# Last FFN's second product in a hybrid trunk: one weight sum moved from DMA to VectorE, another order of work, two token tiles finished earlier

## The chip, the cores and the metric

The kernel runs on one core of a Trainium2 chip. The metric is the device time of one execution in microseconds, from the first to the last instruction and what lies around them; the number for a kernel is the median of several executions. The core has TensorE (PE in the profile, with its weight loads as PEld), VectorE (DVE), ScalarE (ACT), GpSimd (POOL) and SyncE (SP). They run side by side and wait for each other through semaphores. Each takes its own instructions strictly in program order, so an instruction that waits holds up all that stand behind it on the same engine. Transfers (DMA) can be issued from SP, ACT and POOL; only those issued from POOL add into their destination here.

## The reference, cut to what matters

Two layers, 512 tokens, 1024 features. Each layer has a mixer and a SwiGLU FFN, each between two RMS norms with shift, scale and gate. The change is in the last step of the last layer: the FFN's second matrix product, its norm, and the sum into `x`.

```python
D_MODEL = 1024; SEQ = 512; D_FF = 2816
def swiglu_ffn(h, w_in, w_out):
    gate, up = jnp.split(h @ w_in, 2, axis=-1)
    return (jax.nn.silu(gate) * up) @ w_out
...
        y = swiglu_ffn(h, f_w_in[i], f_w_out[i])
        x = x + gate * rmsnorm(y, norm_g[i, 3])
```

All matrix products are done to nearly float32 precision: each operand is split into a high part (a cast on ACT) and a low part (source minus high part, on DVE), and three matmuls stand for one (high by high, low by high, high by low).

## The kernel before, in words

The last second product, (512 x 2816) times (2816 x 1024), is done by a seven-product scheme of the Strassen-Winograd kind instead of eight. The 22 blocks of 128 hidden features are taken as 11 pairs `p`. In a pair the weight rows give four blocks: `b11`, `b12` (first row block, left and right 512 columns) and `b21`, `b22` (second row block). The activations give `a11`, `a12`, `a21`, `a22` (256 tokens each). The seven products, numbered 0 to 6 here, are in `PRODUCTS`, with the accumulator (a pair of PSUM banks `A`, `B`, `C` or `D`, one bank per 128 tokens), the weight block and the activation block:

```python
PRODUCTS = (("A", "b11", "a11"), ("B", "b21", "a12"), ("C", "b22", "a12"), ("A", "b22", "a11"),
            ("D", "b12", "s1"), ("A", "b11", "a21"), ("A", "b21", "a22"))
```

Each product runs over all 11 pairs, so there are 77 steps `(i, p)`, in the order of the list `steps`. Even products take the pairs in the order 0, 1, 2, ... (`even`), odd ones start with pair 4 (`odd`), since there the pairs 0 to 3 come in units of two. Two steps that follow each other make a tile `n`, so there are 39 tiles (0 to 38); a tile is 12 matmuls of 128x512 outputs (`products`, L1785). Tiles 0 to 5 are product 0, tiles 11 to 16 product 2, 16 to 21 product 3, 22 to 27 product 4, 27 to 32 product 5, and 33 to 38 product 6; where a product ends in mid-tile the next begins there. The last three tiles are done for the first 128 tokens of the half, and then for the second 128.

The blocks are changed in place between the products. A unit is a group of pairs that lie in one buffer: units 0 and 1 are the pairs (0, 1) and (2, 3) (512 KB in one block of both), units 2 to 8 the pairs 4 to 10 (256 KB each). The profile calls the buffers of units 0 to 2 `w2t`, those of units 3 and 4 `w2s`, and those of units 5 to 8 `w2h`. For each unit there are four weight sums:

- `t1`: `b12 += b11`, an accumulating DMA from POOL (L1626), before the loop over the tiles.
- `t2_`: `b22 += b12`, an accumulating DMA from POOL. It has to follow the casts of the old `b22` for product 2, and product 3 needs its result.
- `t3`: `b11` becomes the sum of the original `b12` and the original `b22`, for product 5. Before the change `t3_load` reads the original `b12` from memory again, by a DMA issued from ACT (L1796), and `t3` adds the original `b22` from memory by an accumulating DMA issued from POOL.
- `t4`: `b21 += b22`, an accumulating DMA from POOL, for product 6.

All instructions of this part stand in a written order on every engine. The loop over `n` issues `products([n])`, then `behind(n)` (weight sums and the reading of finished accumulators), then `w_prep(n + 4)` and `a_prep(n + 3)`. `w_prep` splits a tile's weights (ACT cast L1750, DVE subtraction L1751, four buffers `whlo`), `a_prep` splits its activations (ACT L1763, DVE L1764, three buffers `ao`). From `n` = 34 on `behind(n)` comes last. Because of the buffers, `w_prep(n + 4)` can start when PE has finished tile `n`.

The four results are read from the banks as products end: `c11` after product 0 and 1, `c12` after 2, 3 and 4 (at `n` = 27), `c22` after 4 and 5 (at `n` = 32, L2032, which has to read bank `A` before product 6 adds to it), and `c21` is what bank `A` holds at the end. `c11` and `c12` belong to the token tiles 0 and 1 of the output, `c21` and `c22` to the tiles 2 and 3. To finish a token tile, ACT squares the two halves and sums along the row (`square`, L1982), DVE forms a mean (`mean`), ACT takes the root and DVE the reciprocal (`root`, L1988 and L1989), DVE multiplies by the gate row (`gated`, L1992), and then forms the new `x` and a DMA stores it (`x_new`, L1998 and L1999).

Of the kernel before, what the change touches and what calls it, by code (L numbers as in the profile page):

```python
# [17 lines left out]
T = 512  # L18
D = 1024
# [12 lines left out]
MUL, ADD, SUB = ALU.mult, ALU.add, ALU.subtract  # L32
# [3 lines left out]
def trunk_kernel(  # L36
# [8 lines left out]
    dma_s = nc.scalar.dma_start  # L45
    act, dve, pe, pool = nc.scalar, nc.vector, nc.tensor, nc.gpsimd
# [16 lines left out]
    def t2(name):  # L63
        return tmp.tile([P, T], F32, tag="t2", name=name, bufs=4)
# [505 lines left out]
    with ExitStack() as ph:  # L570
# [112 lines left out]
        with tc.manual_schedule(engines={PE_ENGINE, mybir.EngineType.SP, mybir.EngineType.Activation,  # L683
# [215 lines left out]
            for k in range(18):  # L899
                i, jp = k % 6, 2 + k // 6 * 2  # L900
# [98 lines left out]
        with tc.manual_schedule(engines={PE_ENGINE, mybir.EngineType.SP, mybir.EngineType.Activation,  # L999
# [15 lines left out]
            for k in range(2 * NF - 6):  # L1015
# [8 lines left out]
                q, j = divmod(k - 3, 4)  # L1024
# [25 lines left out]
    with ExitStack() as ph:  # L1050
# [99 lines left out]
        class Group:  # L1150
# [169 lines left out]
            def root(self):  # L1320
                self.rg = t2("rg")
                act.activation(self.rg, self.ssg, AF.Sqrt, bias=eps_t, scale=1.0 / 256)
# [219 lines left out]
    with ExitStack() as ph:  # L1542
# [4 lines left out]
        NP = NF // 2  # L1547
# [5 lines left out]
        units = [(0, 1), (2, 3)] + [(p,) for p in range(4, NP)]  # L1553
        unit_of = {p: i for i, u in enumerate(units) for p in u}
        rows_of = {}

        def w2_rows(p, n=1):
            return w2[2 * p * P:(2 * p + 2 * n) * P, :].rearrange("(i c p) f -> p i c f", p=P, c=2)
# [10 lines left out]
        def w2_load(i, *names):  # L1569

            u = units[i]
            for name in names:
                r, c = int(name[1]) - 1, int(name[2]) - 1
                dma(b_(i, name), w2_rows(u[0], len(u))[:, :, r, c * T:(c + 1) * T])

        def b_(i, name, q=None):

            t = rows_of[i][int(name[1]) - 1][:, :, slice(0, T) if name[2] == "1" else slice(T, D)]
            return t if q is None else t[:, q, :]
# [45 lines left out]
        def add_(dst, src):  # L1625
            pool.dma_start(dst, src, accum_op=ADD)  # L1626
# [106 lines left out]

        even = list(range(NP))
        odd = [4, 0, 1, 2, 3] + list(range(5, NP))
        steps = [(i, p) for i in range(7) for p in (odd if i % 2 else even)]
        NT = (len(steps) + 1) // 2
        w_of, a_of = {}, {}

# [14 lines left out]
        def a_prep(n):  # L1754
            a = fo.tile([P, 2, 2, 256], F32R, tag="ao", name="ao")
            part = steps[2 * n:2 * n + 2]
            if len(part) == 2 and part[0][0] == part[1][0] and part[1][1] == part[0][1] + 1:
                todo = [(slice(0, 2), part[0], 2)]
            else:
                todo = [(slice(q, q + 1), st, 1) for q, st in enumerate(part)]  # L1760
            for sl, (i, p), m in todo:
                srca = a_(PRODUCTS[i][2], p, m)
                act.copy(a[:, 0, sl, :], srca)  # L1763
                dve.tensor_tensor(a[:, 1, sl, :], srca, a[:, 0, sl, :].bitcast(F32), SUB)  # L1764
            for _, (i, p), m in todo:
                if i == 0:
                    dve.tensor_tensor(a_("a11", p, m), a_("s1", p, m), a_("a11", p, m), SUB)
                elif i == 1:
                    dve.tensor_add(a_("a12", p, m), a_("a12", p, m), a_("a11", p, m))
            a_of[n] = a  # L1770
# [3 lines left out]
        def products(tiles):  # L1774
            for sub in range(2):
                for n in tiles:
                    for q, (i, p) in enumerate(steps[2 * n:2 * n + 2]):
                        r = PRODUCTS[i][0]
                        if r not in bank:
                            bank[r] = [(mm_ps if r == "C" else aux_ps)(f"c{r}{t}") for t in range(2)]  # L1780
                        first = i == {"A": 0, "B": 1, "C": 2, "D": 4}[r] and p == (odd if i % 2 else even)[0]
                        last = p == (odd if i % 2 else even)[-1]
                        w, a, tk = w_of[n], a_of[n], slice(sub * P, (sub + 1) * P)
                        for k, (hl, al) in enumerate(((0, 0), (1, 0), (0, 1))):
                            pe.matmul(bank[r][sub], a[:, al, q, tk], w[:, hl, q, :],  # L1785
                                      start=first and k == 0, stop=last and k == 2, skip_group_check=True)

        with tc.manual_schedule(engines={PE_ENGINE, mybir.EngineType.SP, mybir.EngineType.Activation,
                                         mybir.EngineType.DVE, mybir.EngineType.Pool}):

            def t1(i):
                add_(b_(i, "b12"), b_(i, "b11"))

            def t3_load(i):
                for q, p in enumerate(units[i]):
                    dma_s(b_(i, "b11", q), w2_rows(p)[:, 0, 0, T:])  # L1796

            def t3(i):
                for q, p in enumerate(units[i]):
                    add_(b_(i, "b11", q), w2_rows(p)[:, 0, 1, T:])  # L1800

            def t2_(i):
                add_(b_(i, "b22"), b_(i, "b12"))

            def t4(i):
                add_(b_(i, "b21"), b_(i, "b22"))
# [69 lines left out]
            for u in range(UN):  # L1876
                v = u - 1
                last = u == UN - 1
# [41 lines left out]
            u = UN - 1  # L1920
# [39 lines left out]
            late = range(5, len(units))  # L1960
# [3 lines left out]
            w2_load(4, "b21")  # L1964
            for i in late:
                w2_load(i, "b21")
            for i in (1, 3, 4, *late):
                w2_load(i, "b22", "b12")
            for n in (2, 3):
                w_prep(n)  # L1970
            a_prep(2)
            for i in (0, 2, 1, *range(3, len(units))):
                t1(i)

            st = [{"s2": small(2), "s1": small(1), "b1": small(1)} for _ in range(4)]
# [3 lines left out]
            got = {}  # L1979

            def square(t, part, src):
                act.activation(spare["junk"], src, AF.Square, accum_out=st[t]["s2"][:, part:part + 1])  # L1982

            def mean(t):
                dve.tensor_scalar(st[t]["b1"], st[t]["s2"][:, 0:1], 1.0 / D, EPS, MUL, ADD)
# [5 lines left out]
            def gated(src, hf, dst):  # L1991
                dve.tensor_mul(dst, src, gg[hf])  # L1992
                return dst

            def x_new(t, hf, yg, parts=(FULL,), puts=(dma,)):
                for c, put in zip(parts, puts):
                    cx = slice(hf * T + c.start, hf * T + c.stop)
                    dve.scalar_tensor_tensor(xt[t][:, cx], yg[:, c], st[t]["s1"], xt[t][:, cx], MUL, ADD)  # L1998
                    put(out[0, t * P:(t + 1) * P, cx], xt[t][:, cx])  # L1999

            def behind(n):

                for i, u in enumerate(units):
                    if n - 8 == u[-1] // 2:
                        t2_(i)
                    if n == 13 + i:
                        t3_load(i)
                    if n == 15 + i:
                        t3(i)
                    if n == 18 + i:  # L2010
                        t4(i)
                for t in range(2):
                    if n == 5:
                        got["11", t] = t2("c11")
                        act.copy(got["11", t], bank["A"][t])
                    elif n == 10:
                        dve.tensor_add(got["11", t], got["11", t], bank["B"][t])
                    elif n == 16:
                        got["12", t] = t2("c12")
                        act.copy(got["12", t], bank["C"][t])  # L2020
                    elif n == 21:
                        dve.tensor_tensor(got["12", t], got["12", t], bank["A"][t], SUB)
                    elif n == 27:
                        dve.tensor_add(got["12", t], got["12", t], bank["D"][t])
                        got["22", t] = spare[f"c22_{t}"]
                        act.copy(got["22", t], bank["D"][t])
                    elif n in (29, 30):
                        if t == n - 29:
                            square(t, 0, got["11", t])
                            square(t, 1, got["12", t])  # L2030
                    elif n == 32:
                        dve.tensor_tensor(got["22", t], got["22", t], bank["A"][t], SUB)  # L2032
                    elif n == 34:
                        square(2 + t, 0, got["22", t])
                        mean(t)
                        mean(2 + t)
                    elif n == 35:
                        root(t)
                        gated(got["22", t], 1, got["22", t])
                if n == 35:  # L2040
                    for t in range(2):
                        for hf, c in enumerate(("11", "12")):
                            x_new(t, hf, gated(got[c, t], hf, got[c, t]))

            for n in range(NT - 3):
                products([n])
# [9 lines left out]
                if n >= 34:  # L2056
                    behind(n)
            products(range(NT - 3, NT))
            for t in range(2):
                square(2 + t, 1, bank["A"][t])  # L2060
# [37 lines left out]
```

## Time and profile before

| | before |
|---|---|
| median of 3 runs | 1359.24 us (1358.53 to 1359.59) |
| the profiled execution's own time | 1359.75 us |
| its span, first to last instruction | 1358.0 us |
| mean granted TensorE clock | 0.993 |
| busy: PE, PEld | 1334.3 us (98%), 1147.6 us (85%) |
| busy: DVE, ACT, POOL | 979.6 us (72%), 618.2 us (46%), 74.8 us (6%) |
| stretch 1226 to 1358 us: PE, DVE, ACT, POOL busy | 113.3, 91.8, 69.7, 33.3 us |
| idle of PE before L1785, put down to ACT `ao` L1763 | 15.7 us in 7 waits, weight loads included |

The span is 1.75 us shorter than the execution's own time. The profile's shares are means over many stages; the change lies in the last tenth of the span, so only what this stretch shows bears on it. In a row of a timeline the first number is the start in us from the span's start, the second the length; the text in square brackets is the idle time of that engine just before the row, and what ended it.

### The profile page before, as it was taken

What the parts mean: (1) busy time and instruction counts of PE and PEld (TensorE: products, weight loads), DVE (VectorE), ACT (ScalarE), POOL (GpSimd) and SP (SyncE); (2) the same over time, 40 slices, a digit from 0 to 9 for tenths busy, and PEclk for the clock granted to TensorE, in tenths of its full rate; (3) what the DMA queues carried; (4) which work ended last, traced back from release to release, by engine and by line L of the source; (5) the groups of instructions that cost most, each with busy time, mean ns of one, the idle gap of its engine ahead of it and who ended that gap; (6) DMA issues with size and microseconds to landing.
All of it is one profiled execution on the core that took longest, in us unless ns stands there. A gap on an engine that the chain in (4) does not pass through costs nothing.

```text
span 1358.0 us, 19153 instructions
## 1 busy us (share of the span) xinstructions
PE 1334.3 (98%) x7485; PEld 1147.6 (85%) x7485; DVE 979.6 (72%) x1570; ACT 618.2 (46%) x995; POOL 74.8 (6%) x93
## 2 busy tenths in 40 slices
PE   8999999999999999999999999999999999999986
PEld 7788889888888888898888888888899999998764
DVE  5578866777776322759988898897678777759656
ACT  5333355232223211755555455563574555536554
POOL 0000000000000000000000000000000121101340
PEclk9999999999999999999999999999999999999988
DMA  9757760777776223415443424323434888879891
GB/s 310 236 180 236 240 200 11 242 231 252 225 248 211 99 94 99 122 34 175 122 138 111 125 79 138 109 78 124 139 80 101 210 216 198 209 199 287 187 171 63
DMA packets 203056, 221.69 MB, mean 163 GB/s; under 512 B 8644, under 2 KB 148820, under 8 KB 201940
## 3 DMA queue, kind: packets, MB, share of 16 engines
q1 hardware_dynamic: 186384, 184.74, 43.9%
q0 software_dynamic: 10848, 19.93, 8.7%
q10 hardware_dynamic: 5732, 15.79, 3.7%
q8 instruction: 59, 0.97, 0.3%
q14 instruction: 33, 0.27, 0.1%
HBM read 201.14 MB, written 2.24 MB: 150 GB/s over the span
## 4 chain that ended last, share of the span: by engine, by line
PE 88%; issue 4%; POOL 2%; DMA 2%; SPq 2%; DVE 1%; ACT 1%; POOLq 0%; DVEq 0%; ACTq 0%
PE ip L276 14%; PE ip L278 14%; PE ip L277 14%; PE sA L1694 6%; PE y L378 6%; PE y L379 6%; PE y L380 6%; PE sC L1694 3%; PE li L276 3%; PE li L278 3%; PE li L277 3%; PE sB L1694 2%; PE li L756 1%; PE yd L1283 1%; PE yo L1277 1%
## 5 line engine op out<-in xcount | busy, mean ns | idle before, releaser
L276 PE MATMUL ip<-h,whl 128*128 128x512 f32 x840 | 331.3, 394 | 0.2 <-DVE cv L863 0.2
L278 PE MATMUL ip<-h,whl 128*128 128x512 f32 x840 | 327.2, 390 | 0.0
L277 PE MATMUL ip<-h,whl 128*128 128x512 f32 x840 | 327.0, 389 | 0.0
L276 PEld LDWEIGHTS ip<-h,whl 128*128 128x128 f32 x840 | 157.8, 188 | 33.9 <-issue 1.8
L278 PEld LDWEIGHTS ip<-h,whl 128*128 128x128 f32 x840 | 157.7, 188 | 33.2
L277 PEld LDWEIGHTS ip<-h,whl 128*128 128x128 f32 x840 | 157.8, 188 | 31.8
L222 DVE TENSOR_TENSOR whl<-wst,whl 128x1024 fp32r<-128x1024 f32 x99 | 120.4, 1221 | 60.3 <-ACT whl L221 60.1
L124 DVE SCALAR_TENSOR_TENSOR ada_acc<-ada_st,csil,ada_acc 128x512 f32<-128x512 f32 x140 | 105.0, 750 | 3.5
L204 DVE TENSOR_TENSOR whlo<-wsto,whlo 128x1024 fp32r<-128x1024 f32 x41 | 49.9, 1224 | 78.2 <-ACT whlo L203 78.1
L221 ACT CAST whl<-wst 128x1024 fp32r<-128x1024 f32 x99 | 103.0, 1041 | 4.5 <-DMA wst<-in_m_w_in_dram 2.6
L276 PE MATMUL li<-h,whl 128*128 128x256 f32 x288 | 83.2, 289 | 0.0
L278 PE MATMUL li<-h,whl 128*128 128x256 f32 x288 | 81.6, 283 | 0.0
L277 PE MATMUL li<-h,whl 128*128 128x256 f32 x288 | 81.5, 283 | 0.0
L203 ACT CAST whlo<-wsto 128x1024 fp32r<-128x1024 f32 x41 | 42.6, 1050 | 76.5 <-PE y L380 75.0
L1694 PE MATMUL sA<-tq,whl 128*128 128x256 f32 x576 | 74.6, 283 | 0.3 <-DVE g L1720 0.3
L1785 PE MATMUL cA<-whlo,ao 128*128 128x512 f32 x264 | 66.5, 410 | 7.2 <-ACT ao L1763 4.1
L1694 PEld LDWEIGHTS sA<-tq,whl 128*128 128x128 f32 x576 | 71.6, 192 | 0.6 <-DVE g L1720 0.5
L1785 PEld LDWEIGHTS cA<-whlo,ao 128*128 128x128 f32 x264 | 51.8, 198 | 21.0 <-ACT ao L1763 8.4
L378 PE MATMUL y<-whlo,ff 128*128 128x512 f32 x176 | 68.6, 390 | 0.0
L380 PE MATMUL y<-whlo,ff 128*128 128x512 f32 x176 | 68.5, 389 | 0.0
L379 PE MATMUL y<-whlo,ff 128*128 128x512 f32 x176 | 68.5, 389 | 0.0
L1142 DVE SCALAR_TENSOR_TENSOR cu<-ip,cols,cu 128x511 f32<-128x511 f32 (+2 forms) x84 | 62.8, 747 | 3.9 <-ACT cu L1139 1.4
(328 smaller groups left out, 2442.9 us busy)
## 6 DMA issues: line engine op xcount, KB each, us to landing
ada_st<-in_ada_w_dram SPq DMA_DIRECT2D x96, 512.0 KB, 5.2
wst<-in_f_w_in_dram SPq DMA_DIRECT2D x26, 1024.0 KB, 6.5
wst<-in_m_w_in_dram SPq DMA_DIRECT2D x14, 1024.0 KB, 5.4
wsto<-in_f_w_out_dram SPq DMA_DIRECT2D x10, 1024.0 KB, 5.1
wst<-in_m_w_in_dram SPq DMA_DIRECT2D x20, 512.0 KB, 5.2
wst<-in_a_w_in_dram SPq DMA_DIRECT2D x9, 1024.0 KB, 5.9
wsu<-in_f_w_in_dram SPq DMA_DIRECT2D x17, 512.0 KB, 5.7
csb<-cs_d ACTq DMA_DIRECT2D x8, 1024.0 KB, 5.2
```

Of the source, the lines that this page charges most:

```text
L124: dve.scalar_tensor_tensor(acc, w, csil[:, k:k + 1], acc, MUL, ADD)
L221: later.append((lambda sw=sw, w=w: act.copy(w[:, 0, :nk, :], sw), lambda sw=sw, w=w: dve.tensor_tensor(w[:, 1, :nk, :], sw, w[:, 0, :nk, : ...
L222: lambda sw=sw, w=w: dve.tensor_tensor(w[:, 1, :nk, :], sw, w[:, 0, :nk, :].bitcast(F32), SUB)))
L276: pe.matmul(dst, w_at(w, 0, kk), a[:, 0, sl], start=start, stop=False)
L277: pe.matmul(dst, w_at(w, 0, kk), a[:, 1, sl], start=False, stop=False)
L278: pe.matmul(dst, w_at(w, 1, kk), a[:, 0, sl], start=False, stop=stop)
L378: pe.matmul(pst, a[:, 0, tk], wt[:, 0, kk, :], start=k == 0, stop=False)
L379: pe.matmul(pst, a[:, 0, tk], wt[:, 1, kk, :], start=False, stop=False)
L380: pe.matmul(pst, a[:, 1, tk], wt[:, 0, kk, :], start=False, stop=k == K - 1)
L1142: dve.scalar_tensor_tensor(u[:, sft:], pst[:, :T - sft], w[3 - sft], u[:, sft:], MUL, ADD)
L1694: pe.matmul(dst, w[:, wl, k0 + k, :], moving(q, k, al), skip_group_check=True, start=q in ("P1", "P5", "P2") and k == 0 and i == 0, stop=k ...
L1785: pe.matmul(bank[r][sub], a[:, al, q, tk], w[:, hl, q, :], start=first and k == 0, stop=last and k == 2, skip_group_check=True)
```

## The change

Four things are changed, all in the last second product.

1. `t3` no longer uses DMA. `t2_` has left `b22` equal to the original `b22` plus the original `b12` plus `b11`, so DVE subtracts `b11` from it and writes the result over `b11`. That is one VectorE instruction of 128x512 for each pair, one behind each of the tiles 14 to 24, in the order in which product 5 takes the pairs. The eleven loads issued from ACT and the eleven accumulating DMAs issued from POOL for `t3` are gone, and `t4` of unit `i` is issued behind tile 15 + `i` in place of 18 + `i`.
2. Product 2 takes the pairs in the order 4, 5, 0, 1, 2, 3, 6, ..., and `t2_` follows that order: unit 2 and 3 behind tile 8, unit 0 behind 9, unit 1 behind 10 (before: 0, 1, 2, 3 behind 8, 9, 10, 10).
3. `t1` is issued in the order of units 2, 3, 0, 1, 4, ... (before: 0, 2, 1, 3, 4, ...), and the loads of `b22` and `b12` of unit 3 come before those of unit 1 on SP.
4. The token tiles 0 and 1 are finished in the loop: mean behind tiles 29 and 30, root and gating behind tile 31, `x_new` with its stores behind tile 33. Before, all but the squares stood behind tiles 34 and 35. `c22` is still read behind tile 32.

```diff
-        steps = [(i, p) for i in range(7) for p in (odd if i % 2 else even)]
+        turns = [odd if i % 2 else even for i in range(7)]
+        turns[2] = [4, 5, 0, 1, 2, 3] + list(range(6, NP))
+        steps = [(i, p) for i in range(7) for p in turns[i]]
...
-            def t3_load(i):
-                for q, p in enumerate(units[i]):
-                    dma_s(b_(i, "b11", q), w2_rows(p)[:, 0, 0, T:])
-
-            def t3(i):
-                for q, p in enumerate(units[i]):
-                    add_(b_(i, "b11", q), w2_rows(p)[:, 0, 1, T:])
+            def t3(p):
+                i = unit_of[p]
+                q = units[i].index(p)
+                dve.tensor_tensor(b_(i, "b11", q), b_(i, "b22", q), b_(i, "b11", q), SUB)
...
-            for i in (1, 3, 4, *late):
+            for i in (3, 1, 4, *late):
                 w2_load(i, "b22", "b12")
...
-            for i in (0, 2, 1, *range(3, len(units))):
+            for i in (2, 3, 0, 1, *range(4, len(units))):
                 t1(i)
...
             def behind(n):
 
-                for i, u in enumerate(units):
-                    if n - 8 == u[-1] // 2:
+                if 14 <= n < 14 + NP:
+                    t3(turns[5][n - 14])
+                for i in (2, 3, 0, 1, *range(4, len(units))):
+                    if n == 8 + turns[2].index(units[i][-1]) // 2:
                         t2_(i)
-                    if n == 13 + i:
-                        t3_load(i)
                     if n == 15 + i:
-                        t3(i)
-                    if n == 18 + i:
                         t4(i)
...
                         if t == n - 29:
                             square(t, 0, got["11", t])
                             square(t, 1, got["12", t])
+                            mean(t)
+                    elif n == 31:
+                        root(t)
+                        gated(got["11", t], 0, got["11", t])
+                        gated(got["12", t], 1, got["12", t])
+                    elif n == 33:
+                        x_new(t, 0, got["11", t])
+                        x_new(t, 1, got["12", t])
                     elif n == 32:
                         dve.tensor_tensor(got["22", t], got["22", t], bank["A"][t], SUB)
                     elif n == 34:
                         square(2 + t, 0, got["22", t])
-                        mean(t)
                         mean(2 + t)
                     elif n == 35:
-                        root(t)
                         gated(got["22", t], 1, got["22", t])
-                if n == 35:
-                    for t in range(2):
-                        for hf, c in enumerate(("11", "12")):
-                            x_new(t, hf, gated(got[c, t], hf, got[c, t]))
```

More of the change, by code (lines that the diff above doesn't have):

```diff
@@ L1780, in products @@
                             bank[r] = [(mm_ps if r == "C" else aux_ps)(f"c{r}{t}") for t in range(2)]
-                        first = i == {"A": 0, "B": 1, "C": 2, "D": 4}[r] and p == (odd if i % 2 else even)[0]
-                        last = p == (odd if i % 2 else even)[-1]
+                        first = i == {"A": 0, "B": 1, "C": 2, "D": 4}[r] and p == turns[i][0]
+                        last = p == turns[i][-1]
                         w, a, tk = w_of[n], a_of[n], slice(sub * P, (sub + 1) * P)
```

## The prediction

> **What bounds the kernel now.** I read the page first, for the span and for the engine that is nearly always busy, then PE's timeline over the last product.
>
> ```profile
> span 1358.0 us, 19153 instructions
> PE 1334.3 (98%) x7485; PEld 1147.6 (85%) x7485; DVE 979.6 (72%) x1570; ACT 618.2 (46%) x995; POOL 74.8 (6%) x93
> ...
> 1226.55 14.44 PE L1785 MATMUL cA<-whlo,ao 128*128 128x512 f32 x63
> 1240.83 0.84 PE L1785 MATMUL cB<-whlo,ao 128*128 128x512 f32 x3
> ...
> 1256.47 11.04 PE L1785 MATMUL cC<-whlo,ao 128*128 128x512 f32 x48
> 1268.96 5.64 PE L1785 MATMUL cC<-whlo,ao 128*128 128x512 f32 x15 [1.45 <-ACT ao L1763]
> 1274.44 0.84 PE L1785 MATMUL cA<-whlo,ao 128*128 128x512 f32 x3
> ...
> 1305.87 6.28 PE L1785 MATMUL cA<-whlo,ao 128*128 128x512 f32 x27
> 1315.01 5.49 PE L1785 MATMUL cA<-whlo,ao 128*128 128x512 f32 x12 [2.86 <-ACT ao L1763]
> 1321.72 3.83 PE L1785 MATMUL cA<-whlo,ao 128*128 128x512 f32 x14 [1.22 <-ACT ao L1763]
> ...
> 1331.23 16.84 PE L1785 MATMUL cA<-whlo,ao 128*128 128x512 f32 x66 [2.73 <-DVE w2h L2032]
> ```
>
> PE sets the pace: 63 matmuls start over 14.28 us (1226.55 to 1240.83), 0.2267 each, 2.72 for a tile of 12. The 462 matmuls of the seven products take 104.7 us at that pace and need 121.5 (1226.55 to 1331.23 + 16.84 = 1348.07). The loss lies in two places. Product 2, 63 matmuls from 1256.47 to 1274.44, takes 17.97 in place of 14.28: **3.7 us**. From 1305.87 to the end 129 matmuls take 42.2 in place of 29.4 (129 x 0.2267, and 0.16 for the last to end): **12.8 us**. From PE's end to the end of the span another 9.9 us pass. I then asked ACT's timeline, for ACT is named as the releaser, and the busy table of short windows for the clock (its sixth number after the engines).
>
> ```profile
> 1267.77 0.62 ACT L1750 CAST whlo<-w2t 128x512 fp32r<-128x512 f32 x1 [5.03 <-DMA w2t<-w2t]
> 1268.29 0.61 ACT L1763 CAST ao<-raw 128x512 fp32r<-128x512 f32 x1
> ...
> 1320.53 0.62 ACT L1750 CAST whlo<-w2h 128x512 fp32r<-128x512 f32 x1 [3.01 <-DMA w2h<-in_f_w_out_dram]
> ```
> ```profile
> 1270.00:1271.00 1.00, 1.00 (x3) 0.82 (x3) 0.81 (x1) 1.00 (x4) 0.33 (x1) 0.50 1.11 313
> 1273.00:1274.00 1.00, 1.00 (x6) 0.77 (x5) 0.82 (x2) 0.04 (x1) 0.64 (x1) 0.83 1.11 233
> 1333.00:1335.00 2.00, 2.00 (x7) 1.57 (x6) 0.49 (x1) 0.00 (x0) 0.00 (x0) 0.56 0.00 0
> ```
>
> ACT was idle 5.03 us for the sum `t2_` of unit 2 (`w2t<-w2t`), and behind it stood the activation cast that PE waited for. The late loss is the same chain with another sum: ACT waits for `t3`'s additions (`w2h<-in_f_w_out_dram`, 3.01 us the last time). Each such wait costs twice: after PE's gap the granted clock is 0.50 for some 3.4 us, so 1.7 us more are lost (the rest of the 3.7, and 1331.2 to 1334.7).
>
> **POOL's sums.** Why `t2_` came late is seen in POOL's timeline and, by windows, in the time to landing of its transfers (last number).
>
> ```profile
> 1237.56 1.20 POOL L1626 DMA_DIRECT2D w2t<-w2t  x1 [22.00 <-DMA w2s<-in_f_w_out_dram]
> 1239.02 0.93 POOL L1626 DMA_DIRECT2D w2s<-w2s  x1 [0.26 <-DMA w2s<-in_f_w_out_dram]
> ...
> 1248.16 1.17 POOL L1626 DMA_DIRECT2D w2h<-w2h  x1
> ...
> 1252.90 0.87 POOL L1626 DMA_DIRECT2D w2h<-w2h  x1 [0.77 <-issue]
> 1255.94 1.20 POOL L1626 DMA_DIRECT2D w2t<-w2t  x1 [2.17 <-DVE whlo L1751]
> 1261.33 2.14 POOL L1626 DMA_DIRECT2D w2t<-w2t  x2 [4.19 <-DVE whlo L1751]
> 1266.71 1.76 POOL L1626 DMA_DIRECT2D w2s<-w2s  x2 [3.25 <-issue]
> ```
> ```profile
> w2s<-w2s POOLq DMA_DIRECT2D x1, 256.0 KB, 10.3
> w2h<-w2h POOLq DMA_DIRECT2D x1, 256.0 KB, 4.4
> w2t<-w2t POOLq DMA_DIRECT2D x1, 512.0 KB, 5.0
> ```
>
> The starts follow a rule that I read from these rows: no more than three parts of 256 KB are under way. The one of 1248.16 lands at 1252.6, and the third after it starts at 1252.90; the double one of 1255.94 lands at 1260.9, and the next double starts at 1261.33. (DVE is named as the releaser there; I take it for chance, since 1266.71 fits the rule as well, 5.4 behind the double one of 1261.33.) So singles pass at (4.4 + 0.3)/3 = 1.6 us a part, doubles at (5.0 + 0.3)/2 = 2.65.
>
> **Part 1, `t3` on DVE.** Eleven loads and eleven additions go, and with them the late waits: **-12.8**. They are replaced by eleven DVE instructions like these of 128x512:
>
> ```profile
> 1329.19 0.69 DVE L1751 TENSOR_TENSOR whlo<-w2s,whlo 128x512 fp32r<-128x512 f32 x1
> 1329.80 0.69 DVE L1764 TENSOR_TENSOR ao<-raw,ao 128x512 fp32r<-128x512 f32 x1
> 1330.40 1.28 DVE L2032 TENSOR_TENSOR w2h<-w2h,cA 128x512 f32<-128x512 f32 x2
> ```
>
> 0.60 from start to start. A tile costs DVE 1.2 + 0.6 = 1.8 for its splits; with `t3` 2.4, under PE's 2.72. The new wait (for `t2_`) holds nothing: the cast for product 3, two tiles earlier in the order, needs the same sum. So 0; if DVE had no room left, up to 11 x 0.60 = 6.6. `t4` is issued earlier and has some 20 us of room: 0.
>
> **Parts 2 and 3, the order.** `t2_` of units 2 and 3 is moved ahead of units 0 and 1, which serves the wait of 1267.77. But `t1` of unit 0, done long before in the old order, now stands behind `t1` of unit 3, whose load landed at 1239.0 and now comes some 2 us earlier. POOL then does by the rule: `t1`(3) and `t1`(0) from 1236.5, together 768 KB like the two of 1237.56 and 1239.02, which landed by 1249.3; I take 1248.8. `t1`(1) and (4) to 1253.9 and 1255; `t1`(5) to (8) start between 1254 and 1259; `t2_`(2) 1260.0 to 1264.4, (3) 1260.9 to 1265.3, (0) 1264.7 to 1269.7, (1) 1270.0 to 1275.1, the last, (8), to 1284.5 (the loads of `t3` that ran beside them before are gone). What is needed: tile 16 is due on PE at 1226.55 + 16 x 2.72 = 1270.1, and its activations stand behind the cast of unit 0, so 1.6 us after that sum: 1271.3, a gap of 1.2. Tile 17 likewise behind unit 1: 1276.7 in place of 1274.0, a gap of 2.75, and with the half clock 1.7 more. Units 4 to 8 then come in time. Loss **5.65** in place of 3.7: **+1.95**. Bounds: 2 us earlier or later landing of `t1`(0) shifts it by as much, so 3.5 to 8, and 0 if `t1`(0) finds a free way.
>
> **Part 4, finishing ahead.** The rows are ACT's and DVE's near the end.
>
> ```profile
> 1321.57 0.63 ACT L1982 ACTIVATE w2s<-c 128x512 f32<-128x512 f32 x1
> ...
> 1341.74 1.28 ACT L1988 ACT_TABLE_LOAD   x1
> 1343.03 0.48 ACT L1988 ACTIVATE ss<-ss 128x1 f32<-128x1 f32 x2
> ...
> 1348.11 0.60 ACT L1982 ACTIVATE w2s<-cA 128x512 f32<-128x512 f32 x1 [2.33 <-PE cA L1785]
> ```
> ```profile
> 1344.69 0.69 DVE L1992 TENSOR_TENSOR c<-c,w2h 128x512 f32<-128x512 f32 x1
> ...
> 1353.16 0.75 DVE L1998 SCALAR_TENSOR_TENSOR x<-w2h,ss,x 128x512 f32<-128x512 f32 x1
> 1353.83 0.87 DVE L1998 SCALAR_TENSOR_TENSOR x<-yg,ss,x 128x256 f32<-128x256 f32 x2
> ```
>
> The end: DVE now works off the last of eight gatings and nine pieces of `x_new` and ends at 1354.70, 6.63 after PE; the stores take 3.3 more. Of this, four gatings and four `x_new` move into the loop. What is left after PE: square and its sum 0.75, root 0.3, reciprocal 0.2, `x_new` 0.67 and 0.87, in all 2.85: **-3.8**.
>
> The price is in the loop. Count from PE's start of tile 29; tile 33 is due at 10.9. ACT ends tile 28's casts at 1.8 (from 0.2, three at 0.52), then does two squares (0.75 each) and casts (1.55) for tiles 29 and 30, to 7.7, then the table load (1.28) and the first root: 9.3. DVE waits for that root, does two reciprocals and four gatings (2.65) to 12.05, then the splits behind them (1.8) to 13.85, and only then the first L2032 (0.6), which frees bank `A`: 14.5, so PE starts tile 33 at 14.65, a gap of 3.75, and loses 1.7 more to the half clock: **+5.45**. Without the moved work the gap would be 1.1. The four `x_new` behind tile 33 (2.7) delay splits that are not due for 5 us: 0. Bounds: 1.1 without a half clock, to 7.
>
> **Sum.** 1359.75 - 12.8 + 1.95 + 5.45 - 3.8 = 1350.55 on the profiled execution, which is 0.5 above the median of the runs: **1350.0**.
>
> The clock against the skill: in the rows, 0.50 follows a gap of 1.45 us. The Trainium skill (TensorE: Matmul & The Clock Gate, "Why this matters for your kernels") says that gaps stay harmless up to about 3 us. By it only the gap at tile 33 would slow PE; the trace disagrees with its gap of 1.45.
>
> **The rivals.**
> - *Cool clock only after long gaps*, a mechanism of its own here: the gap of 1.2 after the steady product 2 and that of 2.75 cost no half clock, as the gap of 1.22 at 1321.72 was followed by full speed: 1.7 less, 1348.3. Chance 0.10.
> - *The order works*: `t1`(0) and (1) pass quickly behind the loads and `t2_` is in time. Product 2 and 3 lose 0 to 1: 1345. Against it: the 10.3 us to landing. 0.18.
> - *The finishing hides*: DVE gets through before bank `A` is due, as the bound of 1.1: 4.4 less, 1345.6. Against it: DVE takes its work in order. 0.17.
> - *DVE becomes the bound* over tiles 14 to 24, where `t3` leaves 0.3 a tile: up to 6.6 more, 1353 to 1357. 0.10.
> - *Slower: POOL's sums pass at the doubles' pace.* If all 18 parts from 1248.8 on took 2.65, `t2_`(8) would land at 1296.5 and tile 20, due at 1281, would start at 1297.8 and lose 1.7 to the half clock: a loss of 18.5 in place of 5.65, so 1362.9. It decides from 2.45 us a part. For it: the two doubles now meet in the middle; against: the singles of 1248 to 1253 at 1.6. 0.05.
> - *It doesn't do what it says*: the late gaps are ACT's or DVE's own, and stay: 1350.0 + 12.8 = 1362.8. Against it: ACT's 3.01 for a transfer that no longer exists. 0.02.
>
> The forecast itself has 0.38. **Range** 1343.5 to 1355.5: it takes in both cases that gain 4 to 5 us, parts of both together, and DVE as bound at its middle. Faster by over 0.2% (2.7 us, about what can be told from no change) 0.91, the same 0.02, slower 0.07.
>
> **What would show it.** In the profile after: no ACT wait for `w2h<-in_f_w_out_dram`; no gap from tile 22 to 32; a PE gap near tiles 16 and 17, put down to ACT, with ACT waiting for `w2t<-w2t`; one of 3 to 4 us before tile 33, put down to L2037 of the changed kernel; PE ending near 1342.5 and DVE 2.9 later. It is wrong if product 3 has no gap, if tile 33 starts on time, or if DVE is busy without a break in tiles 14 to 24 while PE waits.

## The result, and the profile after

| | before | after |
|---|---|---|
| median | 1359.33 us | 1351.45 us (1350.9 to 1353.19) |
| ratio to before, 95% interval | | 0.9945 (0.9928 to 0.9962) |
| profiled execution: own time, span | 1359.75, 1358.0 us | 1351.48, 1349.2 us |

The change makes the kernel faster by 0.55%. First the page of the kernel after, then the rows of PE's timeline that answer to those before; the matmuls of the last product are now on line L1787.

```profile
span 1349.2 us, 19124 instructions
PE 1329.8 (99%) x7485; PEld 1145.6 (85%) x7485; DVE 984.9 (73%) x1581; ACT 618.2 (46%) x995; POOL 65.1 (5%) x82
```
```profile
1226.38 14.44 PE L1787 MATMUL cA<-whlo,ao 128*128 128x512 f32 x63
...
1256.30 13.76 PE L1787 MATMUL cC<-whlo,ao 128*128 128x512 f32 x60
1270.93 0.73 PE L1787 MATMUL cC<-whlo,ao 128*128 128x512 f32 x2 [0.87 <-ACT ao L1765]
1272.22 0.50 PE L1787 MATMUL cC<-whlo,ao 128*128 128x512 f32 x1 [0.55 <-DVE ao L1766]
...
1276.52 0.73 PE L1787 MATMUL cA<-whlo,ao 128*128 128x512 f32 x2 [1.73 <-ACT ao L1765]
1277.86 13.45 PE L1787 MATMUL cA<-whlo,ao 128*128 128x512 f32 x58 [0.61 <-DVE ao L1766]
1291.14 14.44 PE L1787 MATMUL cD<-whlo,ao 128*128 128x512 f32 x63
...
1306.78 14.44 PE L1787 MATMUL cA<-whlo,ao 128*128 128x512 f32 x63
1324.92 17.84 PE L1787 MATMUL cA<-whlo,ao 128*128 128x512 f32 x66 [3.70 <-DVE w2h L2037]
```

At 0.2267 us a matmul these rows give the sum. Products 2 and 3 (132 matmuls, 1256.30 to 1291.14) lose 4.92 us; before, the same 132 lost 3.84 (1256.47 to 1290.23). From tile 22 to tile 32 no time is lost: the 63 matmuls of 1306.78 run at full pace, where before the long losses began. PE then waits 3.86 us for DVE's reading of bank `A` (from 1321.06, when the next start was due; the 3.70 in the row counts from the last matmul's end) and takes 17.84 for the last 66, 2.7 more than at full speed. From PE's end (1342.76) to the end of the span it is 6.44, before 9.93. So -12.8 + 1.1 + 6.6 - 3.5, and 0.2 from an earlier start, make the 8.8 us by which the span is shorter.

POOL's timeline in the window of the first loss, and ACT's (with its table load, later on), both of the kernel after:

```profile
1236.79 0.88 POOL L1626 DMA_DIRECT2D w2s<-w2s  x1 [25.40 <-DMA w2t<-in_f_w_out_dram]
1237.45 1.46 POOL L1626 DMA_DIRECT2D w2t<-w2t  x1
1248.47 1.22 POOL L1626 DMA_DIRECT2D w2t<-w2t  x1 [9.56 <-DMA w2h<-in_f_w_out_dram]
...
1259.07 0.86 POOL L1626 DMA_DIRECT2D w2t<-w2t  x1 [0.82 <-DVE whlo L1753]
1260.70 0.86 POOL L1626 DMA_DIRECT2D w2s<-w2s  x1 [0.77 <-DVE whlo L1753]
1263.81 1.22 POOL L1626 DMA_DIRECT2D w2t<-w2t  x1 [2.25 <-DVE whlo L1753]
1269.79 1.20 POOL L1626 DMA_DIRECT2D w2t<-w2t  x1 [4.76 <-issue]
```
```profile
1269.53 1.05 ACT L1752 CAST whlo<-w2t 128x1024 fp32r<-128x1024 f32 x1 [4.89 <-DMA w2t<-w2t]
1274.90 1.04 ACT L1752 CAST whlo<-w2t 128x1024 fp32r<-128x1024 f32 x1 [3.71 <-DMA w2t<-w2t]
...
1318.13 1.28 ACT L1987 ACT_TABLE_LOAD   x1
```

The first sum of unit 3 holds POOL for 25.4 us, unit 0's starts behind it at 1237.45, and unit 1's only when that has landed. (The row of unit 3's sum names a load of `w2t`, which that sum does not read. SP issued the loads that it needs at 1229.1 and those of `w2t` right behind them, at 1230.1; the profile seems to have named the neighbour.) The second sum of unit 2 is in time now; those of units 0 and 1 reach ACT at 1269.5 and 1274.9, too late for tiles 16 and 17.

DVE's timeline around tile 33, and its last row, of the kernel after:

```profile
1319.83 1.27 DVE L1991 TENSOR_TENSOR c<-c,w2h 128x512 f32<-128x512 f32 x2
1321.03 0.15 DVE L1988 RECIPROCAL ss<-ss 128x1 f32<-128x1 f32 x1
1321.10 1.27 DVE L1991 TENSOR_TENSOR c<-c,w2h 128x512 f32<-128x512 f32 x2
...
1323.49 0.69 DVE L1766 TENSOR_TENSOR ao<-raw,ao 128x512 fp32r<-128x512 f32 x1
1324.09 1.28 DVE L2037 TENSOR_TENSOR w2h<-w2h,cA 128x512 f32<-128x512 f32 x2
...
1344.98 0.88 DVE L1997 SCALAR_TENSOR_TENSOR x<-yg,ss,x 128x256 f32<-128x256 f32 x2
```

The four gatings (1319.8 to 1322.3) stand ahead of the splits, and these ahead of L2037, for which PE has been ready since about 1321.2.

### The profile page after: what moved, and what is told of

The parts are those of the page before. It is cut to its first block, busy times and chain, and to the rows that moved or that the text cites. A ratio compares the mean times of both kernels' runs of the same rounds, so it can differ in the third digit from the quotient of the medians.

```text
span 1349.2 us, 19124 instructions
## 1 busy us (share of the span) xinstructions
PE 1329.8 (99%) x7485; PEld 1145.6 (85%) x7485; DVE 984.9 (73%) x1581; ACT 618.2 (46%) x995; POOL 65.1 (5%) x82
## 4 chain that ended last, share of the span: by engine, by line
PE 89%; DMA 4%; DVE 2%; ACT 2%; issue 2%; SPq 1%; POOL 1%; DVEq 0%; POOLq 0%; ACTq 0%
PE ip L276 14%; PE ip L278 14%; PE ip L277 14%; PE sA L1694 6%; PE y L378 6%; PE y L379 6%; PE y L380 6%; PE sC L1694 3%; PE cA L1787 2%; PE li L276 2%; PE li L278 2%; PE li L277 2%; PE li L756 2%; PE sB L1694 1%; PE yd L1283 1%
## 5 line engine op out<-in xcount | busy, mean ns | idle before, releaser
L1787 PE MATMUL cA<-whlo,ao 128*128 128x512 f32 x264 | 64.3, 402 | 6.0 <-DVE w2h L2037 3.7
L1787 PEld LDWEIGHTS cA<-whlo,ao 128*128 128x128 f32 x264 | 51.3, 195 | 18.0 <-issue 4.1
```

Of the source, the lines that this page charges most:

```text
L1787: pe.matmul(bank[r][sub], a[:, al, q, tk], w[:, hl, q, :], start=first and k == 0, stop=last and k == 2, skip_group_check=True)
```

## The experiments

The theory was that one part of the change carries the gain and that the two others cost time, each by a mechanism of its own that can be taken away.

**The third sum alone.** The kernel before, with `t3` on DVE and `t4` behind tile 15 + `i`; orders and finish are the old ones.

```diff
+                if 14 <= n < 14 + NP:
+                    t3(odd[n - 14])
...
-                    if n == 13 + i:
-                        t3_load(i)
                     if n == 15 + i:
-                        t3(i)
-                    if n == 18 + i:
                         t4(i)
```

> The kernel before with one part of the change alone: the third weight sum on VectorE (and the fourth sum issued three tiles earlier, as in the change). Orders of units and the finish are the old ones. My theory: this part carries the whole gain. The 12.8 us lost in products 5 and 6 shrink to a gap of about 1.1 us before tile 33, the rest is as before: about 1347.6, or 1349 to 1350 if the half clock follows that gap. So it is faster than the full change. Rival 1 (VectorE has no room for eleven more instructions): 1352 to 1357, with VectorE busy without a break in tiles 14 to 24 while PE waits. Rival 2 (the new order of units is needed for the gain): no gain beyond 2 us, 1357 to 1359.

Measured: 1347.85 us (1346.52 to 1349.03), ratio 0.9915 (0.9900 to 0.9929). PE's rows:

```profile
1257.03 11.04 PE L1785 MATMUL cC<-whlo,ao 128*128 128x512 f32 x48
1269.74 5.65 PE L1785 MATMUL cC<-whlo,ao 128*128 128x512 f32 x15 [1.67 <-ACT ao L1763]
...
1306.53 14.44 PE L1785 MATMUL cA<-whlo,ao 128*128 128x512 f32 x63
1321.75 15.21 PE L1785 MATMUL cA<-whlo,ao 128*128 128x512 f32 x66 [0.78 <-ACT whlo L1750]
```

The wait of product 2 is the old one (1.67, then the half clock), the late losses are gone, and before tile 33 there is a gap of 0.78 with full speed behind it. One part of the change is worth 11.6 us, more than the whole. This run also issues `t4` three tiles earlier, as the change does; the two were not taken apart. What speaks for `t3` is that ACT's waits before named its additions.

**The old finish.** The full change with token tiles 0 and 1 finished behind tiles 34 and 35, as before.

```diff
-                            mean(t)
-                    elif n == 31:
-                        root(t)
-                        gated(got["11", t], 0, got["11", t])
-                        gated(got["12", t], 1, got["12", t])
-                    elif n == 33:
-                        x_new(t, 0, got["11", t])
-                        x_new(t, 1, got["12", t])
...
+                if n == 35:
+                    for t in range(2):
+                        for hf, c in enumerate(("11", "12")):
+                            x_new(t, hf, gated(got[c, t], hf, got[c, t]))
```

> The full change, but with the old finish of token tiles 0 and 1 (mean, root, gating, new x and stores behind tiles 34 and 35). My theory: the finish in the loop costs more than it brings. Before tile 33 the gap shrinks from 3.9 to 1.1 us and no half clock follows (2.7 us less), while 3.5 us come back after PE's end: about 1349.5, some 2 us faster than the full change. Rival (the gap before tile 33 is of another making, and the finish ahead is pure gain): 1355, with the gap still there.

Measured: 1350.05 us (1348.73 to 1350.61), ratio 0.9930 (0.9913 to 0.9947). By the medians that is 1.4 us below the full change; the two intervals overlap, so this pair of times alone would not settle it, but PE's last row does: the gap of 3.70 is 0.78, and the last 66 matmuls take 15.2.

```profile
1322.49 15.22 PE L1787 MATMUL cA<-whlo,ao 128*128 128x512 f32 x66 [0.78 <-ACT whlo L1752]
```

**The gates later.** Finished ahead of PE's end, but behind the reading of bank `A`.

```diff
-                    elif n == 31:
+                    elif n == 33:
                         root(t)
                         gated(got["11", t], 0, got["11", t])
                         gated(got["12", t], 1, got["12", t])
-                    elif n == 33:
-                        x_new(t, 0, got["11", t])
-                        x_new(t, 1, got["12", t])
...
                     elif n == 34:
+                        x_new(t, 0, got["11", t])
+                        x_new(t, 1, got["12", t])
                         square(2 + t, 0, got["22", t])
```

> The full change, with root and gating of token tiles 0 and 1 moved from behind tile 31 to behind tile 33, and the new x with its stores from behind tile 33 to behind tile 34, so that nothing stands ahead of the reading of bank A. My theory: gap before tile 33 about 1.1 us, no half clock, and the short end of the change is kept: 1351.45 - 2.8 - 2.7 = 1346.0, up to 1346.5 if the end grows a little. Rival (PE waits in tile 33 for something else than VectorE's queue): 1351 as the full change, with the gap still there. Second rival (the moved work now delays the splits for tiles 36 to 38): 1348 to 1350, with a gap of 1 to 3 us near tile 36.

Measured: 1346.00 us (1345.49 to 1348.66), ratio 0.9905 (0.9890 to 0.9921). The gap is 0.78 again, and no other takes its place; DVE ends 3.1 us behind PE (1337.24 to 1340.33). PE's last row and DVE's:

```profile
1321.98 15.26 PE L1787 MATMUL cA<-whlo,ao 128*128 128x512 f32 x66 [0.78 <-ACT whlo L1752]
...
1339.45 0.88 DVE L1997 SCALAR_TENSOR_TENSOR x<-yg,ss,x 128x256 f32<-128x256 f32 x2
```

**Unit 0's first sum early.** Tests the rule that I read from POOL's starts.

```diff
-            for i in (2, 3, 0, 1, *range(4, len(units))):
+            for i in (2, 0, 3, 1, *range(4, len(units))):
                 t1(i)
```

> The full change, with the first weight sums issued in the order of units 2, 0, 3, 1, 4 and on, so that unit 0 no longer stands behind unit 3's late load. My theory (three parts of 256 KB at most under way from POOL): unit 0's first sum lands near 1220 again, the second sums of units 2, 3, 0, 1 start near 1254, 1256, 1259 and 1264 (full change: 1259.1, 1260.7, 1263.8, 1269.8), those of units 0 and 1 land near 1264 and 1269, in time for tiles 16 and 17, and the 4.9 us lost in products 2 and 3 go: 1346.5. Rival (the second sums are late for another reason, the loads or VectorE): the starts stay within 1 us of the full change's and the time at 1351.

Measured: 1346.59 us (1346.06 to 1347.60), ratio 0.9906 (0.9892 to 0.9921). The second sums of units 2, 3, 0 and 1:

```profile
1255.05 0.86 POOL L1626 DMA_DIRECT2D w2t<-w2t  x1 [1.36 <-DVE ao L1766]
1255.94 0.86 POOL L1626 DMA_DIRECT2D w2s<-w2s  x1
1259.11 1.22 POOL L1626 DMA_DIRECT2D w2t<-w2t  x1 [2.31 <-DVE whlo L1753]
1264.46 1.20 POOL L1626 DMA_DIRECT2D w2t<-w2t  x1 [4.14 <-DVE whlo L1753]
```

1254, 1256, 1259 and 1264 were expected. PE's one gap in products 2 and 3 is at tile 17:

```profile
1273.96 13.44 PE L1787 MATMUL cA<-whlo,ao 128*128 128x512 f32 x58 [0.51 <-DVE ao L1766]
```

The two products lose 0.8 us (1256.52 to 1287.24), where they lost 3.84 before the change. So the new order of units does help, when unit 0 isn't put behind unit 3.

**Doubles split.** The same bytes in the change's own order, with single transfers.

```diff
-                add_(b_(i, "b12"), b_(i, "b11"))
+                for q in range(len(units[i])):
+                    add_(b_(i, "b12", q), b_(i, "b11", q))
...
-                add_(b_(i, "b22"), b_(i, "b12"))
+                for q in range(len(units[i])):
+                    add_(b_(i, "b22", q), b_(i, "b12", q))
```

> The full change in its own order, but the first and second weight sums of units 0 and 1 are issued as two transfers of 256 KB each in place of one of 512 KB; the bytes are the same. My theory (three parts of 256 KB at most under way, so that two doubles never overlap while three singles do): 18 parts at 1.6 us; the second sums of unit 0 land near 1266 and those of unit 1 near 1269 (full change: 1269.5 and 1274.9), the gaps at tiles 16 and 17 go, and the time is 1346.5 to 1347.5. Rival (the transfers are bound by bytes or by the memory loads, not by how many are under way): landings within 1 us of the full change's, 1351.

Measured: 1346.33 us (1344.98 to 1346.80), ratio 0.9898 (0.9882 to 0.9915). POOL's rows for the second sums of units 0 and 1:

```profile
1259.33 0.87 POOL L1626 DMA_DIRECT2D w2t<-w2t  x1 [0.76 <-DVE whlo L1753]
1260.78 0.87 POOL L1626 DMA_DIRECT2D w2t<-w2t  x1 [0.58 <-issue]
1262.32 0.86 POOL L1626 DMA_DIRECT2D w2t<-w2t  x1 [0.68 <-DVE ao L1766]
1263.77 0.86 POOL L1626 DMA_DIRECT2D w2t<-w2t  x1 [0.59 <-issue]
```

The four parts of units 0 and 1 start 1.5 us apart, where the two doubles of the full change start 6 us apart (1263.81 and 1269.79) for the same bytes. It is the number under way that binds, and not the bytes: with each transfer counted from its start to its landing, 256 KB as one part, POOL has three parts under way again and again from 1200 us on, and never more, in all ten kernels of this document. What sets that number is open: no run here has another one.

**Both mends**, the later gates and unit 0 early:

> The full change with both mends: first weight sums in the order of units 2, 0, 3, 1, 4 and on, and root and gating of token tiles 0 and 1 behind tile 33, their new x behind tile 34. My theory (the two losses are independent, since one lies in products 2 and 3 and the other before tile 33): 1351.45 - 4.9 - 5.45 = 1341.1. Rival (both feed the same wait, so that one mend takes the other's gain): 1345 to 1346, no better than the better of the two alone.

Measured: 1342.32 us (1341.49 to 1342.45), ratio 0.9866 (0.9851 to 0.9881). The two losses are independent, within about 1 us. The gap of 0.61 at tile 17 and that of 0.78 at tile 33 are left:

```profile
1274.03 13.48 PE L1787 MATMUL cA<-whlo,ao 128*128 128x512 f32 x58 [0.61 <-DVE ao L1766]
...
1318.21 15.27 PE L1787 MATMUL cA<-whlo,ao 128*128 128x512 f32 x66 [0.78 <-ACT whlo L1752]
```

**The third sum three times**, on top of both mends: is its cost nothing, or only hidden?

```diff
-                dve.tensor_tensor(b_(i, "b11", q), b_(i, "b22", q), b_(i, "b11", q), SUB)
+                for _ in range(3):
+                    dve.tensor_tensor(b_(i, "b11", q), b_(i, "b22", q), b_(i, "b11", q), SUB)
```

> The version with both mends, with the third weight sum's VectorE instruction issued three times in a row (each time weight minus result, so that the value stays the same up to rounding). Does its cost stay hidden only because a tile leaves VectorE 0.3 us? My theory: 1.8 + 3 x 0.6 = 3.6 us of VectorE for a tile against PE's 2.72 in tiles 14 to 24, so 0.88 x 11 = 9.7, and about 1 for the reading of bank A behind tile 21, less the lead of about 2.7 us that the splits have: PE loses 7 to 8 us there, in gaps put down to VectorE or to the casts behind it, 1348 to 1349. Rival (VectorE's order leaves far more cover): within 2 us of the version with both mends.

Measured: 1355.41 us in one execution, 13.1 above both mends and well beyond the 7 to 8 expected. PE's tiles now start 3.86 us apart, each behind a wait for DVE, and DVE is busy 27.5 of the 28 us from 1272 to 1300. The timelines of PE and DVE, and the table of windows (DVE is the third number with a count):

```profile
1277.63 3.01 PE L1787 MATMUL cA<-whlo,ao 128*128 128x512 f32 x12 [0.83 <-DVE ao L1766]
1281.49 3.02 PE L1787 MATMUL cA<-whlo,ao 128*128 128x512 f32 x12 [0.85 <-DVE ao L1766]
...
1277.49 2.13 DVE L1800 TENSOR_TENSOR w2t<-w2t 128x512 f32<-128x512 f32 x3
```
```profile
1272.00:1300.00 28.00, 22.58 (x91) 16.06 (x89) 27.52 (x42) 15.03 (x27) 11.13 (x12) 1.00 0.83 141
```

Two things were wrong in that expectation. The three depend on each other and take 2.05 in place of 1.80. And the lead of 2.7 us that the splits were to have isn't there, for the casts before them had just waited for unit 1's second sum. Price and room were right in kind: 1.8 + 2.05 = 3.85 against 2.72.

**Split and later gates together**, as the version without the two losses:

> The full change in its own order of first sums, with the transfers of units 0 and 1 split into singles, and with root and gating behind tile 33 and the new x behind tile 34. My theory: the split removes the whole loss in products 2 and 3 (4.9 us), the later gating the 5.45 us around tile 33: 1351.45 - 4.9 - 5.45 = 1341.1, and the last 0.6 us that the version with both mends still loses at tile 17 go too: 1341 to 1342, at or below the version with both mends. Rival (with no waits left, the splits on VectorE fall behind by the third sum in tiles 17 to 24): 1343 to 1345, with gaps put down to VectorE in tiles 18 to 24.

Measured: 1340.84 us (1340.73 to 1341.00), ratio 0.9863 (0.9846 to 0.9879): the fastest by its median, though its interval overlaps that of both mends. Products 2 to 5 run without a gap, and 0.77 us before tile 33 is all that is left:

```profile
1271.84 14.44 PE L1787 MATMUL cA<-whlo,ao 128*128 128x512 f32 x63
...
1316.97 15.27 PE L1787 MATMUL cA<-whlo,ao 128*128 128x512 f32 x66 [0.77 <-ACT whlo L1752]
```

## Why the prediction was right

*The third sum, -12.8 forecast.* -12.8 in the rows of the full change, and 11.6 by the medians for that part alone. Right, with its cover as worked out: 2.4 us of DVE a tile (the splits of two tiles start at 1280.73 and 1283.13) under 2.72. The thrice-run kernel shows how thin that cover is.

*The order, +1.95 forecast.* +1.1. The chain of starts was right to about 1 us (second sums of units 2, 3, 0, 1 at 1259.1, 1260.7, 1263.8 and 1269.8; forecast 1260.0, 1260.9, 1264.7, 1270.0), and so were the starts of tiles 16 and 17. The step that failed is the half clock behind the second gap: its 1.7 us did not come in this execution. The sum missed by less than that, since it left something out as well: behind the first matmuls of each of the two tiles PE waits once more, for DVE's half of the split (0.55 and 0.61 in the rows). So the gaps alone cost 4.9 us, where 1.2 + 2.75 = 3.95 had been worked out. Two windows of the full change, behind tile 17's gap and behind tile 33's (the granted clock is the third number from the end):

```profile
1276.00:1279.00 3.00, 1.88 (x7) 1.26 (x8) 3.00 (x5) 3.00 (x7) 2.04 (x3) 1.00 0.86 144
...
1324.00:1330.00 6.00, 5.08 (x12) 4.09 (x13) 5.83 (x10) 0.00 (x0) 0.00 (x0) 0.50 0.22 81
```

*The finish in the loop, +5.45 and -3.8 forecast.* +6.6 and -3.5. The gap was 3.86 for a forecast of 3.75. The waits on the way came out within some 0.2 us, two slips of the sum included (1.8 and twice 3.05 make 7.9 and not 7.7; 9.3 and 2.65 make 11.95 and not 12.05). The mis-sized term is the half clock behind the gap, at 2.7 in place of 1.7: it began at 1323.6, in the gap itself, and lasted to 1330.4, twice as long as the 3.4 us that the prediction took. At the end DVE stops 3.1 us behind PE, for 2.85 worked out. That the gap and the half clock come from the gatings' place is shown by the two kernels that moved them.

*The rivals and the sum.* "The order works" and "the finishing hides" did not come true as the change stands, but each did when one line or one place was altered, at 1346.6 and 1346.0 (1345 and 1345.6 were worked out for them). "DVE becomes the bound" did not happen with one instruction, and did with three. "Cool clock only after long gaps" was right about tile 17 in this execution and wrong as a rule, as the next paragraph shows. The span shrank by 8.8 us for 9.2 forecast. That it came so near is in part luck: one half clock too many (1.7) stood against the waits left out (1.0) and the second half clock's extra 1.0. Of the 1.4 us between 1350.0 and 1351.45 another 0.5 lies outside the span (2.3 us in place of 1.75), and the runs of the change spread by 2.3.

*The clock rule.* In the full change gaps up to 1.73 stayed at full speed, as the Trainium skill has it (TensorE: Matmul & The Clock Gate, "Why this matters for your kernels"), against my reading. But the kernel with later gates has the same pair of gaps (1.70 and 0.61) and was granted half speed behind it (its window, the clock in the same place):

```profile
1276.00:1279.00 3.00, 2.54 (x6) 2.05 (x7) 3.00 (x6) 2.49 (x6) 1.24 (x2) 0.50 1.05 178
```

So the length of a gap does not decide alone, and the limit of about 3 us in the Trainium skill did not protect a shorter gap here. The same page of the Trainium skill ("What's actually happening") says that the activity window runs freely and is not reset when a kernel starts.

The traces agree. In all ten, each stretch at one clock between two changes lasts a whole multiple of 3.41 us. In the kernel before, the clock falls at 1269.92, rises at 1273.33, falls at 1314.29, rises at 1321.12, falls at 1331.36 and rises at 1334.77, so the stretches between are 1, 12, 2, 3 and 1 times 3.41. The changes lie on a grid that the gaps do not shift. Cut along that grid, the two kernels differ. The first row is of the kernel with later gates, the other two of the full change; the number behind the length is PE's busy time:

```profile
1272.61:1276.02 3.41, 1.54 (x6) 0.62 (x4) 1.44 (x2) 2.52 (x5) 2.28 (x3) 1.00 0.83 142
1272.42:1275.83 3.41, 2.37 (x10) 1.60 (x9) 0.68 (x2) 0.93 (x1) 0.70 (x2) 1.00 1.06 180
1275.83:1279.25 3.42, 2.13 (x8) 1.47 (x9) 3.27 (x5) 3.42 (x8) 2.46 (x4) 1.00 0.84 141
```

With later gates the gap of 1.70 lies within one window; in the full change a border at 1275.83 cuts the gap of 1.73 in two. From 1258 us on, in all ten traces, every window of 3.41 us at full clock with PE busy for 1.99 us or more was followed by full clock, and every one with 1.54 or less by half. Between them both came: half after 1.67 and 1.89, full after 1.70, 1.69 and 1.82 (the first with the old finish, the others with the third sum three times). So what counts lies near half a window busy; PE's busy time alone does not fix it. The price at tile 33 fits as well: in the full change PE works at half clock from 1324.92 to 1330.45, and half of these 5.53 us is 2.76, for 2.72 measured.

## What to carry to other kernels

Price a change part by part from the stage where each part lies: here one part was worth more than the whole, and the two others could be mended by moving a few lines. Before work is moved forward on an engine, look for the instruction behind it in program order that frees a buffer or bank; four gatings cost some 5.5 us (1351.45 against 1346.00) because the reading of one bank stood behind them. And read a queue's starts against the landings of earlier transfers: if only so many can be under way, their order, and whether they are split, can count more than their bytes. Give a gap on TensorE a range of prices: one pair of gaps was followed by half clock in one kernel, at some 1.4 us, and by none in another, with the borders of the clock's windows falling elsewhere.

## What the runs showed of the hardware

- Accumulating transfers from POOL: from 1200 us on, at most three parts of 256 KB are under way in any of the ten traces. 512 KB as one transfer passed at some 2.65 us for 256 KB, as two at 1.5.
- The half clock behind one and the same gap of 3.7 us before tile 33 cost 2.7 us in the full change, 2.7 with unit 0 early (17.83 for 66 matmuls), and 1.5 with the doubles split (16.65): it is not a fixed price. In the first two the half clock lasted 6.83 us, in the third 3.41.
- The granted clock changes only on a grid of 3.41 us. From 1258 us on, every window of that length at full clock with PE busy for at most 1.54 us was followed by half clock, and none with 1.99 or more; between them both were seen.
- VectorE starts 128x512 float32 instructions 0.60 us apart when they are independent, and 0.72 apart when each needs the one before: three such, and an independent one 0.61 behind the last, make the 2.05 of the thrice-run kernel.
